# A hybrid diffusion layer on one core: the first stage in another order, with four tiles unnormalized and part of the first loads split

## The chip, the cores and the metric

The kernel runs on one core of a Trainium2 chip. The core has five engines with queues of their own: TensorE (PE in the profile, with its weight loads as PEld), VectorE (DVE), ScalarE (ACT), GpSimd (POOL) and SyncE (SP), which issues nearly all the loads. Sixteen DMA engines move the data. The metric is the device time of one execution, in microseconds. The kernel before takes 1244.59 us, the median of 3 runs (1243.99 to 1247.25).

## What is computed

One layer of a diffusion backbone over 512 latent tokens (`x`, 512 × 1024) and 256 context tokens, in float32. Its first part, which is all that the change touches, is the modulated RMS norm and the product of its result with columns of one wide matrix `w_in`:

```
def rmsnorm(x, g):
    y = x32 * lax.rsqrt(jnp.mean(x32 * x32, axis=-1, keepdims=True) + EPS)
    return y * g

def modulate(x, g, shift, scale):
    return rmsnorm(x, g) * (1 + scale) + shift

mod = jax.nn.silu(c) @ w_mod[l] + b_mod[l]            # 6 x 1024 numbers: shift, scale, gate, twice
sh1, sc1, gt1, sh2, sc2, gt2 = jnp.split(mod[:, None, :], N_MOD, axis=-1)
h_lat = modulate(x, norm1_g[l], sh1, sc1)
p_lat = h_lat @ w_in                                  # and the same for the context, with c_ctx
```

The rest (a bidirectional Mamba-2 scan, windowed attention, two branch gates, an output projection, a convolutional feed-forward network, a last RMS norm) comes after and is the same in both kernels.

## The kernel before

**Layout.** The stream is kept transposed, with channels on the 128 partitions: `x` is eight tiles of 128 channels × 512 tokens (`xs_[:, j, :]`, j from 0 to 7), the context eight tiles of 128 × 256 (`xc_`). A float32 product is made of three matmuls on rounded parts: with w = hi + lo and x = hi + lo it adds hi·hi, hi·lo and lo·hi. `split` (lines 148 to 150) makes the parts of a weight tile: a cast on ACT and a subtraction on DVE.

**The first stage** (lines 297 to 523) does three things at once. It makes shift and scale from `c` and the 8 MB of `w_mod`; it normalizes `x` and the context; and meanwhile it already multiplies `x` with the first 640 columns of the gates (`w0`, eight tiles of 128 × 640), which accumulate in five banks of PSUM, `pg[0]` to `pg[4]`.

**Unnormalized tiles.** The norm's factor r of a token is known only when the squares of all eight tiles are summed. A token's factor can be put after the product, however: with a = g·(1 + scale), h = x·a·r + s. For the first `NU` = 3 tiles, `scaled` (line 396) makes only x·a (`ah` on ACT, `al` on DVE), and the products go into the banks without r. When r is there, `scale_banks` (line 444) multiplies the five banks by it in place, on DVE, and the other tiles are added normalized (`norm`, line 388: `xsb` on DVE, `hlh` on ACT, `hll` on DVE). The shift's part of the unnormalized tiles, s·w0, is added up apart by `shifts` (line 412) in `pbias` and goes into the bias of the gates (`bias_rows`, `bias_cols`). Later products need all eight tiles normalized, so the first three are normalized too, at the end of the stage (`N0` to `N2`).

**The factor.** `squares` (line 381) squares tiles on ACT and adds them up on DVE in `ssq`, one after another. Each square is pinned (`keep_in_program_order`) behind the instruction that ACT was given just before it in the text. `sums` adds over the partitions by eight one-column matmuls on PE (line 237), adds eps on DVE, and takes the power −0.5 on POOL (line 248); `spread` spreads r over the partitions by transposes on PE (line 254), and ACT copies it into SBUF (line 273).

**The order.** PE's order is written out by hand, in the string `order`. Its words, for a tile j: `Aj` (`mod_rows`, line 352) are 16 narrow matmuls with two tiles of `w_mod`, a copy `tm` on ACT, and the split of the w0 tile j; `Bj` (`mod_cols`) are four small matmuls, after which ACT makes `a` and `s`; `Hj` (`prep`) is `scaled` or `norm`; `Pj:xy` are the products of tile j into the banks x to y−1, three matmuls each; `Zj` is `shifts`; `sq_*` are squares; `hold` and `keep` are matmuls whose result nobody reads. The other engines' queues, SP's among them, are ordered by a scheduler from the text's order and a model of the times; nothing but the pins is written by hand there.

**Loads.** SP issues the loads in the text's order. w_mod comes in 16 tiles of 512 KB in six buffers, w0 in eight tiles of 320 KB in four buffers, x in four loads of two tiles (512 KB), `vec` (all vectors by channel: 360 columns, 180 KB) in one load. Columns 0 to 55 of `vec` hold the bias of the modulation and the first norm's weights, which `a` and `s` need; columns 88 and up are read by `half` (line 445), which halves them for later stages.

After the stage, `k_step`, `q_step` and `v_step` multiply the normalized tiles (lines 193 to 196), and PE goes on without a break.

Of the kernel before, what the change touches and what calls it, by code (L numbers as in the profile page):

```python
# [20 lines left out]
L = 512  # L21
# [8 lines left out]
V_N2 = 56  # L30
V_FG = 64
V_SG = 72
V_CW = 88
# [3 lines left out]
NV = 360  # L37


def raw(ap):  # L40
    return ap.bitcast(F32)
# [3 lines left out]
def tile_hybrid_layer(  # L45
# [32 lines left out]
    nc = tc.nc  # L78
    V, S, G, T = nc.vector, nc.scalar, nc.gpsimd, nc.tensor
# [36 lines left out]
    def tmp(tag):  # L116
        return tpool.tile([P, 512], F32, tag=tag, name=tag, bufs=TMP[tag])
# [84 lines left out]
    vec = cpool.tile([P, NV], F32, name="vec")  # L202
# [9 lines left out]
    half = cpool.tile([P, NV - V_CW], F32, name="half")  # L212
# [72 lines left out]
    ssq = hpool.tile([P, L], F32, name="ssq")  # L285
# [8 lines left out]

    NU, NG = 3, 5
    first = {}
    gates = []
    with tc.tile_pool(name="spool", bufs=1) as sp:  # L300
        xs_ = sp.tile([P, KT, L], F32, name="xsb")
# [9 lines left out]
        def load_mod(i):  # L311
            t = sp.tile([P, 4, 256], F32, tag="wm", name="wm", bufs=6)
            nc.sync.dma_start(t, wm1[i].rearrange("p (k c) -> p k c", k=4))
            return t

        def load_w0(j):
            r = sp.tile([P, 640], F32, tag="w0", name="w0", bufs=4)
            nc.sync.dma_start(r, w0[j])
            return r

        def load_x(k):
            nc.sync.dma_start(xs_[:, 2 * k : 2 * k + 2, :], xT[k].rearrange("p (k t) -> p k t", k=2))

        nc.sync.dma_start(ccs, cc)
        mod_raw = {i: load_mod(i) for i in range(2)}
        nc.sync.dma_start(ident, ident_d)
        nc.sync.dma_start(vec, vecs)
        w0_raw = {0: load_w0(0)}
        load_x(0)
        for j in (1, 2):  # L330
            mod_raw.update({i: load_mod(i) for i in (2 * j, 2 * j + 1)})
            w0_raw[j] = load_w0(j)
            load_x(j)
        load_x(3)
        G.memset(raw(still), 1.0)
        G.memset(csil32, 0.0)
        G.memset(s32, 0.0)
# [43 lines left out]
        def squares(x_, q, n, ks):  # L381
            for k in ks:
                sq = tmp(("ta", "tb")[k % 2])[:, :n] if k else q
                tc.keep_in_program_order(S.activation(sq, x_[:, k, :], AF.Square))
                if k:
                    V.tensor_tensor(q, q, sq, ALU.add)
# [50 lines left out]
        def spread(x, n):  # L437
            r[x] = in_sbuf(rms_spread(r[x], n, new=accb), n, "r_" + x)

        def hold(n):  # L440
            for _ in range(n):
                T.matmul(unread[:, :256], still[:, :P], still, start=True, stop=True)

        def scale_banks():
            V.tensor_scalar_mul(half, vec[:, V_CW:NV], 0.5)
            for i in range(NG):
                V.tensor_tensor(pg[i], pg[i], r["l"], ALU.mult)

        def bias_rows():
# [15 lines left out]
        def load_next():  # L465
# [9 lines left out]
        rows = {}  # L475
# [5 lines left out]
            "N": lambda j: norm(j, 0, xs_, r["l"], hlh, hll),  # L481
        }
        calls = {
            "sq_0": lambda: squares(xs_, ssq, L, range(2)),
            "sq_1": lambda: squares(xs_, ssq, L, range(2, 4)),
            "sq_2": lambda: squares(xs_, ssq, L, range(4, 5)),
            "sq_3": lambda: squares(xs_, ssq, L, range(5, 8)),
            "hold": lambda: hold(18),
            "keep": lambda: hold(6),
            "sq_c": lambda: squares(xc_, cq, LC, range(4)),  # L490
# [2 lines left out]
            "sum_c": lambda: sums("c", cq, 2),  # L493
            "put_l": lambda: spread("l", 4),
            "put_c": lambda: spread("c", 2),
            "scale": scale_banks,
            "rows": bias_rows,
            "cols": bias_cols,
            "ctx": load_ctx,
# [2 lines left out]


        order = """
            hold A0 keep B0 H0 sq_0 keep Z0 P0:02 A1 P0:24 B1 H1 sq_1 P0:45 P1:01 A2 sq_2 P1:13 B2 H2 sq_3 P1:35 Z1 P2:01 sum_l A3
            P2:13 B3 put_l H3 P2:35 Z2 scale A4 rows ctx P3:02 B4 H4 cols P3:24 A5 sq_c P3:45 B5 H5 P4:03 A6 P4:35 B6 H6 sq_d
            P5:03 A7 N0 P5:35 B7 H7 P6:02 sum_c N1 P6:25 put_c N2 P7:05 next
        """
        with tc.manual_schedule(engines={mybir.EngineType.PE}):
            for what in order.split():  # L510
                if what in calls:
                    calls[what]()
                elif what[0] == "P":
                    j = int(what[1])
# [1628 lines left out]
```

## Time and profile before

| what | us |
|---|---|
| median of the runs | 1244.59 |
| the profiled execution | 1244.94 |
| its span, first to last instruction | 1243.1 |
| mean granted clock of TensorE | 0.996 of full |
| first product of the first stage (PE, line 409) | 10.37 |
| `sum_l` (PE, line 237) | 26.00 |
| `r_l` copied (ACT, line 273) | 32.07 |
| last products into the banks (PE, line 409), from | 59.76 |

The span is one execution, taken by the hardware profiler; the execution's own time has 1.8 us more around it. A row of the timeline gives the start, the duration, the engine, the line, the operation with the names of the output and inputs, the shapes, how many were merged (x4), and in brackets the idle time before it and who ended it. Matmuls are pipelined, so their durations overlap: the distance from one start to the next tells what one costs. The granted clock is the share of full speed at which TensorE was allowed to run in a window.

### The profile page before, as it was taken

Reading aid. Unit: us, or ns where it says so; the run is one execution under the profiler, and the core shown is the slowest. Engines: PE = TensorE matmul, PEld = TensorE weight load, DVE = VectorE, ACT = ScalarE, POOL = GpSimd, SP = SyncE. Lnnn points to the kernel's source line nnn. Section 1 sums busy time; section 2 is a strip of 40 time slices with the busy share of each in tenths; the row PEclk is TensorE's granted clock in tenths of the full one; section 3 lists DMA queues with packets and bytes.
Section 4 is the critical chain, followed back from the end, with each engine's and each line's share of the span. In section 5 each row is a group of like instructions: output and inputs, shape, how many; then the busy total and the mean of one; then the engine's idle time right before and its main releaser. Section 6 shows DMA issues by size and latency. Waiting matters only on the chain.

```text
span 1243.1 us, 17448 instructions
## 1 busy us (share of the span) xinstructions
PE 1219.0 (98%) x6322; PEld 997.8 (80%) x6322; DVE 922.0 (74%) x1482; ACT 685.5 (55%) x1302; POOL 168.9 (14%) x174
## 2 busy tenths in 40 slices
PE   8999999999999999998999999999999999999997
PEld 5798888888878877777777678888988888888885
DVE  3846887888565698697886986567688787886556
ACT  4657887888546457467375563223545444445543
POOL 0000111111100033242351630000200000000000
PEclk9999999999999999999999999999999999999998
DMA  9653568867848334446346457667154444456785
GB/s 372 224 154 87 186 197 197 229 179 208 226 153 242 114 96 125 128 133 175 125 136 220 127 185 245 197 207 240 50 170 155 145 144 153 152 171 242 246 309 184
DMA packets 108342, 224.65 MB, mean 181 GB/s; under 512 B 9440, under 2 KB 48672, under 8 KB 108256
## 3 DMA queue, kind: packets, MB, share of 16 engines
q1 hardware_dynamic: 100768, 197.32, 48.9%
q0 software_dynamic: 6912, 25.17, 8.6%
q8 instruction: 50, 0.82, 0.3%
q10 hardware_dynamic: 576, 1.05, 0.2%
q14 instruction: 36, 0.29, 0.1%
HBM read 193.29 MB, written 49.87 MB: 196 GB/s over the span
## 4 chain that ended last, share of the span: by engine, by line
PE 73%; DVE 13%; DMA 5%; ACT 5%; issue 2%; POOL 0%; SPq 0%; POOLq 0%; ACTq 0%; DVEq 0%
PE acc L193 17%; PE acc L196 17%; PE acc L194 17%; PE po L843 3%; PE score L794 3%; PE pt L830 2%; DMA wraw<-wt_d 2%; DMA wraw<-wdn 2%; PE mis L409 2%; DVE wlo L150 2%; DVE E L1450 1%; PE acc L913 1%; PE acc L915 1%; PE acc L914 1%; PE mis L1385 1%
## 5 line engine op out<-in xcount | busy, mean ns | idle before, releaser
L193 PE MATMUL acc<-hlh,whi 128*128 128x512 f32 x488 | 199.3, 408 | 0.7 <-ACT te L684 0.7
L149 ACT CAST whi<-wraw 128x1024 fp32r<-128x1024 f32 (+2 forms) x119 | 122.8, 1033 | 132.4 <-PE acc L194 94.9
L150 DVE TENSOR_TENSOR wlo<-wraw,whi 128x1024 fp32r<-128x1024 f32 (+2 forms) x119 | 143.4, 1205 | 69.4 <-ACT whi L149 64.5
L196 PE MATMUL acc<-hlh,wlo 128*128 128x512 f32 x488 | 191.4, 392 | 0.0
L194 PE MATMUL acc<-hll,whi 128*128 128x512 f32 x488 | 190.7, 391 | 0.0
L193 PE MATMUL acc<-mh,whi 128*128 128x512 f32 x360 | 141.0, 392 | 0.0
L196 PE MATMUL acc<-mh,wlo 128*128 128x512 f32 x360 | 140.1, 389 | 0.0
L194 PE MATMUL acc<-ml,whi 128*128 128x512 f32 x360 | 140.1, 389 | 0.0
L196 PEld LDWEIGHTS acc<-hlh,wlo 128*128 128x128 f32 x488 | 91.6, 188 | 20.2
L193 PEld LDWEIGHTS acc<-hlh,whi 128*128 128x128 f32 x488 | 91.9, 188 | 18.4 <-issue 2.2
L194 PEld LDWEIGHTS acc<-hll,whi 128*128 128x128 f32 x488 | 92.0, 188 | 17.5 <-issue 1.7
L194 PEld LDWEIGHTS acc<-ml,whi 128*128 128x128 f32 x360 | 67.6, 188 | 14.5 <-issue 0.5
L193 PEld LDWEIGHTS acc<-mh,whi 128*128 128x128 f32 x360 | 67.6, 188 | 14.4 <-issue 0.5
L196 PEld LDWEIGHTS acc<-mh,wlo 128*128 128x128 f32 x360 | 67.6, 188 | 14.0
L803 DVE CUSTOM_DVE_ANT_0 p<-score,winm,nsink 128x512 f32<-128x512 f32 (+1 forms) x64 | 51.8, 810 | 16.2 <-PE score L794 14.7
L1251 DVE SCALAR_TENSOR_TENSOR ta<-acc,half,ta 128x511 f32<-128x511 f32 (+1 forms) x66 | 43.8, 663 | 23.7 <-ACT ta L1250 23.7
L810 ACT ACTIVATE p<-p,mneg 128x512 f32<-128x512 f32 (+1 forms) x64 | 49.7, 777 | 15.4 <-DVE mneg L803 14.8
L1370 POOL TENSOR_TENSOR st<-st,eT 128x512 f32<-128x512 f32 x24 | 33.5, 1397 | 172.9 <-DMA wraw<-wm 106.2
L1250 ACT ACTIVATE ta<-acc,half 128x512 f32<-128x512 f32 (+1 forms) x66 | 46.6, 705 | 16.4 <-PE acc L196 15.1
L193 PE MATMUL acc<-hch,whi 128*128 128x256 f32 x176 | 54.4, 309 | 0.0
L838 DVE TENSOR_TENSOR ptl<-pt,pth 128x512 fp32r<-128x512 f32 x72 | 47.5, 685 | 8.6 <-ACT pth L834 7.8
L566 DVE SCALAR_TENSOR_TENSOR tm<-wraw,csil,tm 128x512 f32<-128x512 f32 x56 | 45.1, 805 | 10.7 <-DMA wraw<-wm 9.9
(501 smaller groups left out, 2950.4 us busy)
## 6 DMA issues: line engine op xcount, KB each, us to landing
wraw<-wup SPq DMA_DIRECT2D x44, 512.0 KB, 3.6
wt_d<-wdn POOLq DMA_DIRECT2D x36, 512.0 KB, 7.6
fb<-cs_d SPq DMA_DIRECT2D x32, 512.0 KB, 5.5
wraw<-wm SPq DMA_DIRECT2D x32, 512.0 KB, 3.6
wraw<-wx SPq DMA_DIRECT2D x24, 512.0 KB, 4.2
wraw<-wt_d SPq DMA_DIRECT2D x20, 512.0 KB, 4.2
sp_d<-te SPq DMA_DIRECT2D x33, 256.0 KB, 2.1
wm<-wm SPq DMA_DIRECT2D x16, 512.0 KB, 8.3
```

What stands on the lines that cost most here:

```text
L149: S.copy(hi[:, :n], r[:, :n])
L150: V.tensor_tensor(lo[:, :n], r[:, :n], raw(hi[:, :n]), ALU.subtract)
L193: T.matmul(ps, wh, xh[:, k0 + k, :], start=a, stop=False)
L194: T.matmul(ps, wh, xl[:, k0 + k, :], start=False, stop=False)
L196: T.matmul(ps, wl, xh[:, k0 + k, :], start=False, stop=b)
L566: V.scalar_tensor_tensor(acc, r[:, u * 512 : u * 512 + 512], sc, acc, ALU.mult, ALU.add)
L794: T.matmul(ps[:, o : o + len(z) * P], Q[h][:, b * P : (b + 1) * P], k[:, j, z[0] * P : (z[-1] + 1) * P], start=v == 0 and o % 512 in (0, P ...
L803: V.tensor_tensor_reduce(p[:, :w], d["ps"][i][:, o0 : o0 + w], m, op0=ALU.add, op1=ALU.min, scale=1.0, scalar=nsink[:, h : h + 1], accum_o ...
L810: S.activation(p, p, AF.Exp, bias=d["mneg"][:, i : i + 1], scale=-1.0, accum_out=d["den"][:, i : i + 1])
L838: V.tensor_tensor(d["ptl"][x], d["pt"][x], raw(d["pth"][x]), ALU.subtract)
L1250: S.activation(o[:, :n], ps[:, :n], AF.Identity, scale=hcol(base_w, stride + i), bias=hcol(base_b, i))
L1251: V.scalar_tensor_tensor(o[:, 1:n], ps[:, 0 : n - 1], hcol(base_w, i), o[:, 1:n], ALU.mult, ALU.add)
```

## The change

`NU` goes from 3 to 4: tile 3 is unnormalized too, has its shifts (`Z3`), and is normalized at the end (`N3`). The first two x tiles are loaded singly, the others in pairs as before; of `vec`, the first 56 columns are loaded where all were, and the rest behind the last x tile. The squares are cut otherwise (1, 1, 2 and 4 tiles instead of 2, 2, 1 and 3), and the last four, `sq_3`, stand behind `H3`. The sum `sum_l` stands behind `P3:02`, which is behind `A3`; before it stood ahead of `A3`. The scaling of the banks is in two parts, `half` is a step of its own, and the context's load (`ctx`) moves from behind `A4` to behind `A6`.

```diff
-    NU, NG = 3, 5
+    NU, NG = 4, 5
...
+        def load_tile(k):
+            nc.sync.dma_start(xs_[:, k, :], xT[k // 2, :, k % 2 * L : k % 2 * L + L])
+
         nc.sync.dma_start(ccs, cc)
         mod_raw = {i: load_mod(i) for i in range(2)}
         nc.sync.dma_start(ident, ident_d)
-        nc.sync.dma_start(vec, vecs)
+        nc.sync.dma_start(vec[:, :V_N2], vecs[:, :V_N2])
         w0_raw = {0: load_w0(0)}
-        load_x(0)
-        for j in (1, 2):
-            mod_raw.update({i: load_mod(i) for i in (2 * j, 2 * j + 1)})
-            w0_raw[j] = load_w0(j)
-            load_x(j)
+        load_tile(0)
+        mod_raw.update({i: load_mod(i) for i in (2, 3)})
+        w0_raw[1] = load_w0(1)
+        load_tile(1)
+        mod_raw.update({i: load_mod(i) for i in (4, 5)})
+        w0_raw[2] = load_w0(2)
+        load_x(1)
+        load_x(2)
         load_x(3)
+        nc.sync.dma_start(vec[:, V_N2:], vecs[:, V_N2:])
...
-        def scale_banks():
-            V.tensor_scalar_mul(half, vec[:, V_CW:NV], 0.5)
-            for i in range(NG):
+        def scale_banks(banks):
+            for i in banks:
                 V.tensor_tensor(pg[i], pg[i], r["l"], ALU.mult)
...
-            "sq_0": lambda: squares(xs_, ssq, L, range(2)),
-            "sq_1": lambda: squares(xs_, ssq, L, range(2, 4)),
-            "sq_2": lambda: squares(xs_, ssq, L, range(4, 5)),
-            "sq_3": lambda: squares(xs_, ssq, L, range(5, 8)),
+            "sq_0": lambda: squares(xs_, ssq, L, range(1)),
+            "sq_1": lambda: squares(xs_, ssq, L, range(1, 2)),
+            "sq_2": lambda: squares(xs_, ssq, L, range(2, 4)),
+            "sq_3": lambda: squares(xs_, ssq, L, range(4, 8)),
...
-            "scale": scale_banks,
+            "half": lambda: V.tensor_scalar_mul(half, vec[:, V_CW:NV], 0.5),
+            "scale_a": lambda: scale_banks(range(2)),
+            "scale_b": lambda: scale_banks(range(2, NG)),
...
         order = """
-            hold A0 keep B0 H0 sq_0 keep Z0 P0:02 A1 P0:24 B1 H1 sq_1 P0:45 P1:01 A2 sq_2 P1:13 B2 H2 sq_3 P1:35 Z1 P2:01 sum_l A3
-            P2:13 B3 put_l H3 P2:35 Z2 scale A4 rows ctx P3:02 B4 H4 cols P3:24 A5 sq_c P3:45 B5 H5 P4:03 A6 P4:35 B6 H6 sq_d
-            P5:03 A7 N0 P5:35 B7 H7 P6:02 sum_c N1 P6:25 put_c N2 P7:05 next
+            hold A0 keep B0 H0 sq_0 keep Z0 P0:02 A1 P0:23 B1 H1 sq_1 P0:35 A2 P1:02 B2 H2 sq_2 P1:25 Z1 P2:02 A3 P2:23 B3 H3 sq_3
+            P2:35 Z2 P3:02 sum_l P3:23 A4 put_l P3:34 B4 H4 P3:45 scale_a Z3 scale_b rows A5 half P4:02 cols P4:23 B5 H5 P4:35 A6 ctx sq_c P5:02 B6 H6
+            P5:24 A7 sq_d N0 P5:45 B7 H7 P6:02 sum_c N1 P6:25 put_c N2 P7:03 N3 P7:35 next
         """
```

## The prediction, on record before the changed kernel was run

> **What bounds the kernel now.** I start at the page: the span and the share of each engine.
>
> ```profile
> span 1243.1 us, 17448 instructions
> ...
> PE 1219.0 (98%) x6322; PEld 997.8 (80%) x6322; DVE 922.0 (74%) x1482; ACT 685.5 (55%) x1302; POOL 168.9 (14%) x174
> ```
>
> TensorE (PE) is busy 1219.0 of 1243.1 us, so removing every wait would save 24 us at most, and a gain made early is kept only if nothing else becomes late behind it. Next I read who waited for whom, for PE alone (total us, times, longest).
>
> ```profile
> PE mis L1278 <- DVE tc L1259: 6.0, 3, 2.4
> PE acc L237 <- DVE ssq L386: 2.1, 1, 2.1
> ```
>
> The first row is a later stage, which the change leaves alone. The second is the one large wait of the first stage: `sum_l` (line 237) waits for the last addition to the sum of squares. Then the timeline of PE there (start, duration, idle before).
>
> ```profile
> 22.36 0.63 PE L418 MATMUL acc<-w,s 128*32 128x256 f32 x6
> 22.91 0.50 PE L409 MATMUL mis<-ah,w0h 128*128 128x512 f32 x1
> 23.25 0.39 PE L409 MATMUL mis<-al,w0h 128*128 128x512 f32 x1
> 23.48 0.40 PE L409 MATMUL mis<-ah,w0l 128*128 128x512 f32 x1
> 26.00 1.02 PE L237 MATMUL acc<-rmsc,ssq 128*128 128x1 f32 x8 [2.12 <-DVE ssq L386]
> 26.95 1.07 PE L361 MATMUL acc<-wm,csil 128*32 128x256 f32 x16
> 27.95 0.82 PE L409 MATMUL mis<-ah,w0h 128*128 128x512 f32 x2
> ```
>
> The last product of `P2:01` starts at 23.48, the next product at 27.95. Between them lie the wait, one-column sums and the narrow matmuls of A3. The windows show what follows (busy us of PE, PEld, DVE, ACT, POOL, then granted clock, DMA share, GB/s):
>
> ```profile
> 20.00:30.00 10.00, 7.88 (x52) 5.38 (x51) 5.15 (x8) 4.24 (x10) 1.02 (x1) 0.92 1.03 418
> 28.00:32.00 4.00, 4.00 (x19) 3.50 (x16) 0.00 (x0) 0.88 (x3) 0.39 (x1) 0.57 1.02 417
> 32.70:56.30 23.60, 23.44 (x161) 16.21 (x160) 22.06 (x37) 15.95 (x38) 1.62 (x1) 1.00 0.63 226
> 56.30:64.40 8.10, 8.10 (x38) 6.61 (x37) 6.62 (x16) 5.64 (x13) 0.00 (x0) 1.00 0.37 127
> ```
>
> From 28 to 32 the granted clock was 0.57: 4 × 0.43 = 1.7 us of PE's work was lost. From 32.7 on it is full and PE hardly idles, but VectorE (DVE) is nearly full too, 22.06 of 23.60 us. So before 32.7 PE waits and is slowed, and after it two engines are full.
>
> **The first tile.** Its chain on ScalarE (ACT), before:
>
> ```profile
> 8.31 0.35 ACT L372 ACTIVATE a<-acc,bp,vec 128x2 f32<-128x2 f32 x1 [0.85 <-PE acc L371]
> 8.56 0.25 ACT L373 ACTIVATE s<-acc,vec 128x2 f32<-128x2 f32 x1
> 8.71 0.72 ACT L149 CAST w0h<-w 128x640 fp32r<-128x640 f32 x1
> 9.59 0.72 ACT L400 ACTIVATE ah<-xsb,a 128x512 fp32r<-128x512 f32 x1 [0.16 <-DMA xsb<-xT]
> ```
>
> The change takes 152 KB of vectors and 256 KB of x out of the queue ahead of the first x tile, 1.0 us at 417 GB/s. But `ah` idled only 0.16 us for x: it stands behind `a`, `s` and `w0h`, and `a` waited for PE. So the first product, which follows the end of `ah` at 10.31, starts 0.16 us earlier, near 10.2 (1.0 at the most, if `w0h` went first).
>
> **The load that comes next.** A3 needs w_mod tiles 6 and 7. Tile 7, before (its issue, then its time to landing):
>
> ```profile
> L313 SPq DMA_DIRECT2D wm<-wm x1: 327/327/327, 14.1 to 14.1; - x1
> ...
> DMA to landing us min/median/max: 10.5/10.5/10.5
> ```
>
> It landed at 14.1 + 10.5 = 24.6, with the DMA engines full (share 1.03 above). The new order puts the same bytes ahead of it: every x tile and both parts of `vec` are still issued first. SP issues two DMAs more, and the first vectors come in rows of 224 bytes; both cost nothing as long as PE is at A3 before the load. What PE needs until then I price by the chain that ended last:
>
> ```profile
> 46.30 0.34 PE acc L371 x4
> 46.64 2.21 PE mis L409 x9
> 48.85 1.00 PE acc L361 x16
> ```
>
> A product costs 0.245, an A 1.0, a B 0.35, and six shift matmuls 0.55 (22.36 to 22.91 above). Ahead of A3 now stand P0, P1 and `P2:02`, 36 products, 8.8; A1 and A2 2.0; B1 and B2 0.7; Z1 0.55; and 0.4 in the first tile, whose low half comes late: 12.45. PE is ready at 10.2 + 12.45 = 22.7 and waits until **24.6**. The earlier first tile, be it 0.16 or 1.0 us, is swallowed there. A3 moves from 26.95 to 24.6: **−2.35**. Behind A3 now stands `sum_l` (1.0), and 3 products (0.74) have gone ahead of it: **+0.3**. Z3 is new: **+0.55**.
>
> **The sum of squares.** Each square is pinned behind the instruction that ACT was given before it, so the first of `sq_3` stands behind `ah` of H3. In the kernel before, four additions stood behind `ah` of H2 in the same way:
>
> ```profile
> 20.42 0.50 PE L371 MATMUL acc<-sel,tm 128*128 128x2 f32 x4
> ...
> 21.35 0.72 ACT L400 ACTIVATE ah<-xsb,a 128x512 fp32r<-128x512 f32 x1
> ...
> 25.16 0.69 DVE L386 TENSOR_TENSOR ssq<-ssq,tb 128x512 f32<-128x512 f32 x1
> ```
>
> From B2 (20.42) over `ah` and the last addition to `sum_l` (26.00) it took 5.58 us, however busy PE was. After, B3 comes at 24.6 + 1.0 + 0.74 = 26.35, so `sum_l` can start at 31.9. PE has B3 0.35, `P2:35` 1.47, Z2 0.55 and `P3:02` 1.47 to do and is there at 30.2. So **a wait returns, 1.7 us**, where 2.3 went. Its length is set by the way B3, H3, squares, additions, not by the load. Ends: 0 if the squares came before `ah`, 2.3 as before.
>
> **The clock.** The stretch without a wide product was 23.7 to 27.95, 4.2 us. There are now two, 22.7 to 25.6 (2.9) and 30.2 to 32.9 (2.7). I take it that neither halves the clock: **−1.7** (ends 0 and −1.7). An A behind products, 1.0 us without a wide one (48.85 above), leaves the clock full (1.00 from 32.7 on), so the point lies between 1.0 and 4.2; 2.9 is inside, and this is rival 1. [...]
>
> **Where the factor is used.** Rows of the timeline, then of the view of the x tiles (ns min/median/max):
>
> ```profile
> 32.07 0.59 ACT L273 COPY r_l<-acc 128x512 f32<-128x512 f32 x1 [0.41 <-PE acc L254]
> ...
> 33.36 1.29 DVE L447 TENSOR_TENSOR mis<-mis,r_l 128x512 f32<-128x512 f32 x2
> ```
>
> ```profile
> L391 DVE SCALAR_TENSOR_TENSOR xsb<-xsb,a,r_l x8: 744/745/751, 32.7 to 53.4; 128x512 f32<-128x512 f32 x8
> L392 ACT ACTIVATE hlh<-xsb,s x8: 707/724/726, 33.6 to 54.3; 128x512 fp32r<-128x512 f32 x8
> L393 DVE SCALAR_TENSOR_TENSOR hll<-xsb,s,hlh x8: 743/744/752, 34.6 to 55.3; 128x512 fp32r<-128x512 f32 x8
> ```
>
> `sum_l` 31.9 to 32.9, three products, A4 to 34.65, `put_l` some 0.4, and the copy of 0.59 half a microsecond later: `r_l` is there at 36.15, against 32.66. B4 starts at 35.05 + 0.74 = 35.8 and a4, 0.9 later (B2 at 20.42 to `ah` at 21.35), is ready at 36.7. PE comes to `P4:02` after `P3:45` 0.74, Z3 0.55, A5 1.0: 38.45. One bank is scaled first (0.645), then `xsb` 0.745 to 37.55, `hlh` to 38.3, in time; `hll` stands behind another bank and ends at 39.1 to 39.75, where the second two products want it at 38.95: 0.2 to 0.8, I take **+0.5**. `half` (0.3 us) and the two parts of the scaling otherwise lie beside products.
>
> **The end of the stage.** What DVE does behind `r_l` stays the same (22.06 us of the window), less one split of 0.82, which now goes ahead, plus `half` 0.3: 21.5. It begins 3.5 us later, so it cannot end before 36.15 + 21.5 = 57.7, where it ended at 56.3; with the 1.5 us of idle as before, 59.2. The context tiles need 8.1 us more (third row to fourth), less the 0.6 they waited there: 66.7. The products of the context began at
>
> ```profile
> 65.24 0.28 PE L193 MATMUL acc<-hch,whi 128*128 128x256 f32 x1
> 65.36 0.28 PE L194 MATMUL acc<-hcl,whi 128*128 128x256 f32 x1
> ```
>
> and start 0.12 us apart, three for a tile, so the eighth tile was wanted at 65.24 + 7 × 0.36 = 67.8, and 1.0 us earlier by the sum so far: 66.8. The cover that was 3.4 us wide (64.4 to 67.8) is gone to nothing. Cost 0 to 1.5 us, I take **+0.3**, as the sums meet almost exactly. N3 is no new work: the same three instructions were H3's; only `ah` and `al` of the fourth tile are new, before `r_l`, where DVE has room (5.15 of 10 us in the first window). On SP the context's load now stands behind that of w0 tile 7, whose buffer Z3 frees only at 37.4, and ahead of w_mod tiles 14 and 15: 2368 KB at 417 GB/s are 5.8 us, 43.2, while A7 comes near 47.7 (from 38.45 on: 27 products, cols, A6, B5, B6 and the 0.5), so 4.5 us of cover are left for its landing. Behind the stage the same products follow, so I carry the shift to the end.
>
> **Sum.** −2.35 + 0.3 + 0.55 + 1.7 − 1.7 + 0.5 + 0.3 = −0.7 us. The profiled execution took 1244.94 us around its span of 1243.1; the median of the runs shown is 1244.59. I set −0.7 against the median: **1243.9 us**. About 0.3%, 3.7 us, is what a measurement of this kernel can tell from no change.
>
> **Rivals.**
> 1. *The clock is halved again.* For it: two stretches of nearly 3 us, close to each other. Against: both are shorter than the 4.2 us that did it. It decides if 2.7 to 2.9 us without wide products are enough. Price 1.7 us for one stretch, 1245.6, or 3.4 for both, 1247.3: slower than before.
> 2. *The load is no bound.* If w_mod tile 7 landed by 22.7, A3 would not wait, 1.9 less: 1242.0. Against: the same bytes ahead of it at a full share. For: the landing is that of the last of 16 engines, which need not lag as far again.
> 3. *The second wait does not come.* If ACT takes the squares before `ah` of H3 (the x tiles are long there), 1.7 less: 1242.2. Against: the pin. Under 2 or 3 the factor comes earlier, and the +0.5 and +0.3 may go too; both together give 1239.5.
> 4. *`half` blocks DVE*, which runs its queue in order. Before, it ran 26 us ahead of its place in the text (beside the scaling at 33.36):
>
> ```profile
> 7.44 0.30 DVE L445 TENSOR_SCALAR half<-vec 128x272 f32<-128x272 f32 x1
> ```
>
> The rest of `vec` now lands two w_mod tiles and one w0 tile ahead of 24.6; 1344 KB at 418 GB/s are 3.3 us, so 21.3. If `half` stands ahead of `al` of tile 1 on DVE, that `al` ends at 21.3 + 0.3 + 0.75 = 22.35 instead of near 17, PE's second products of P1 come 5.2 us late, of which the 1.9 us of slack at A3 take a part: 3.3, and 1.7 for the clock after such a gap: 1248.9, slower. Against: the square of x tile 4 stands before H2 in the text and went behind it, so the order did not count on that tile landing early.
>
> That the first rows come earlier and bring nothing is not a rival but part of the forecast.
>
> **Chances.** The forecast 0.45 (1242.5 to 1245.2, from the ends of the +0.5, the +0.3 and the 5.58 us); rival 1 0.23; rival 2 0.13; rival 3 0.12; rival 4 0.07. Faster by over 0.3%, below 1240.9, are the halves of rivals 2 and 3 in which the other terms go too: 0.14. Slower, above 1248.3, are rival 4 (0.06) and the part of rival 1 in which more than two windows are slow (0.04): 0.10. Within: 0.76. The range takes in both prices of rival 1 and leaves out rival 4 and the lower part of 2 and 3: 1240.5 to 1247.3.
>
> **What would show it.** In the profile after: A3's first matmul near 24.6 with a wait for `wm` (wrong if it starts by 23.2); a wait of `sum_l` for `ssq` near 30 to 32 of 1.7 us; a granted clock of 1.00 from 22 to 36 (rival 1: a stretch of 0.5); `r_l` near 36 and `xsb` of tile 4 at 36.8; DVE full from 36 to 59; the first context product near 64. The first product near 10.2. `half` on DVE behind `al` of tile 2. I would be wrong altogether if products behind the stage, not the stage, moved by more than a microsecond.

## The result and the profile after

| what | before, us | after, us |
|---|---|---|
| median of 6 runs each | 1245.08 | 1256.88 |
| lowest and highest | 1243.99, 1247.25 | 1251.23, 1257.38 |
| the profiled execution, its span, its mean granted clock | 1244.94, 1243.1, 0.996 | 1251.23, 1249.0, 0.995 |
| first product of the first stage | 10.37 | 10.41 |
| `sum_l` | 26.00 | 31.84 |
| `r_l` copied, from | 32.07 | 35.28 |
| `sum_c` | 53.13 | 57.05 |
| first context product (line 193) | 65.24 | 71.04 |

The changed kernel is slower: the ratio of the times, taken over all runs, is 1.0082, with an interval from 1.0063 to 1.0102 (the quotient of the two medians alone is 1.0095; the ratios below are taken over all runs too). The forecast was 1243.9 with a range up to 1247.3, so the time lies 9.6 us above that range.

Two facts say where to look. In the profiled executions the first context product moved by 71.04 − 65.24 = 5.80 us and the span by 1249.0 − 1243.1 = 5.9: what stands behind the stage took 1177.9 us before and 1178.0 after, so in these two executions the loss is in the first stage. And the profiled execution of the changed kernel is the shortest of its six. The others have spans of 1251.7 to 1255.2 at a mean clock of 0.990 to 0.992; span times clock is 1242 to 1244 in all six. So most of what the median lost beyond this profile is lost clock, not longer waits.

The page after:

```profile
span 1249.0 us, 17457 instructions
...
PE 1221.5 (98%) x6328; PEld 997.9 (80%) x6328; DVE 921.9 (74%) x1483; ACT 686.7 (55%) x1303; POOL 168.7 (14%) x174
```

PE is busy 2.5 us more (1219.0 before), for a span 5.9 us longer. Line numbers of the stage are 7 higher than before in what follows (416 was 409, 393 was 386); the helper's line 237 is the same, and later stages are 8 higher (1286 was 1278). The waits of PE after (total us, times, longest):

```profile
PE mis L1286 <- DVE tc L1267: 6.5, 3, 2.4
PE acc L237 <- DVE te L393: 4.3, 1, 4.3
PE acc L237 <- DVE ssq L393: 2.0, 1, 2.0
```

The third row is the wait at `sum_l` that the forecast said would return. The second is new: `sum_c`, the sum over the context's squares, waits 4.3 us for its last addition. Before, `sum_c` did not wait. PE's timeline at both places:

```profile
23.41 0.64 PE L368 MATMUL acc<-wm,csil 128*32 128x256 f32 x8
24.35 0.64 PE L368 MATMUL acc<-wm,csil 128*32 128x256 f32 x8 [0.30 <-DMA wm<-wm]
24.92 0.50 PE L416 MATMUL mis<-ah,w0h 128*128 128x512 f32 x1
...
31.84 1.02 PE L237 MATMUL acc<-rmsc,ssq 128*128 128x1 f32 x8 [1.98 <-DVE ssq L393]
...
52.08 0.63 PE L416 MATMUL mis<-hlh,w0l 128*128 128x512 f32 x2
57.05 0.98 PE L237 MATMUL acc<-rmsc,te 128*128 128x1 f32 x4 [4.33 <-DVE te L393]
57.89 1.63 PE L416 MATMUL mis<-hlh,w0h 128*128 128x512 f32 x3
...
71.04 0.28 PE L193 MATMUL acc<-hch,whi 128*128 128x256 f32 x1
```

and the same word before:

```profile
53.13 0.50 PE L237 MATMUL acc<-rmsc,te 128*128 128x1 f32 x4
```

PE was ready for `sum_c` at 57.05 − 4.33 = 52.72, against 53.13 before: up to here the change had gained 0.4 us. Then it waited 4.33. Why the addition was late is read from ACT and DVE. ACT after:

```profile
50.04 0.38 ACT L370 COPY tm<-acc 128x256 f32<-128x256 f32 x1 [0.36 <-PE acc L368]
50.31 1.05 ACT L149 CAST whi<-wraw 128x1024 fp32r<-128x1024 f32 x1
51.26 0.73 ACT L149 CAST w0h<-w 128x640 fp32r<-128x640 f32 x1
51.88 0.42 ACT L391 ACTIVATE ta<-xcb 128x256 f32<-128x256 f32 x1
...
52.82 0.40 ACT L391 ACTIVATE tb<-xcb 128x256 f32<-128x256 f32 x1
```

ACT before:

```profile
48.84 0.40 ACT L384 ACTIVATE ta<-xcb 128x256 f32<-128x256 f32 x1
...
49.76 0.40 ACT L384 ACTIVATE tb<-xcb 128x256 f32<-128x256 f32 x1
```

These are the first and the last of the four squares of `sq_d`. The new order has it behind `A7`, where it was ahead of `P5:03 A7`, and each square is pinned behind the instruction that stands before it in ACT's text. So the first is now pinned behind the cast `w0h` of A7, which itself comes behind the copy `tm` that waits for A7's matmuls (50.04), and it starts 51.88 − 48.84 = 3.04 us later. DVE after:

```profile
51.44 1.22 DVE L150 TENSOR_TENSOR wlo<-wraw,whi 128x1024 fp32r<-128x1024 f32 x1
52.57 0.82 DVE L150 TENSOR_TENSOR w0l<-w,w0h 128x640 fp32r<-128x640 f32 x1
53.31 0.42 DVE L393 TENSOR_TENSOR te<-te,ta 128x256 f32<-128x256 f32 x1
53.64 0.74 DVE L398 SCALAR_TENSOR_TENSOR xsb<-xsb,a,r_l 128x512 f32<-128x512 f32 x1
54.30 0.42 DVE L393 TENSOR_TENSOR te<-te,tb 128x256 f32<-128x256 f32 x1
54.64 0.74 DVE L400 SCALAR_TENSOR_TENSOR hll<-xsb,s,hlh 128x512 fp32r<-128x512 f32 x1
55.30 0.42 DVE L393 TENSOR_TENSOR te<-te,ta 128x256 f32<-128x256 f32 x1
55.81 0.75 DVE L400 SCALAR_TENSOR_TENSOR hll<-xsb,s,hlh 128x512 fp32r<-128x512 f32 x1
56.48 0.42 DVE L393 TENSOR_TENSOR te<-te,tb 128x256 f32<-128x256 f32 x1
```

DVE before, its last of the four:

```profile
51.22 0.43 DVE L386 TENSOR_TENSOR te<-te,tb 128x256 f32<-128x256 f32 x1
```

DVE is full here: two splits (1.22 and 0.82) stand ahead of the first addition, where before `wlo` stood behind the last, and the four additions of 0.42 stand among norm steps of 0.74. The last one ends at 56.90 against 51.65 before, 5.25 later: 3.04 from ACT's queue and 2.2 from DVE's. Before, 1.48 us of cover lay between that end and `sum_c` (51.65 to 53.13). PE now comes 0.41 earlier, and 0.15 pass from the last addition to `sum_c` (56.90 to 57.05): 5.25 − 1.48 + 0.41 + 0.15 = 4.33, the wait. What then happens to the clock (busy us of PE, PEld, DVE, ACT, POOL, then granted clock, DMA share, GB/s):

```profile
52.00:54.00 2.00, 0.71 (x4) 0.23 (x2) 2.00 (x4) 2.00 (x7) 0.00 (x0) 1.00 0.23 35
54.00:56.00 2.00, 0.00 (x0) 0.00 (x0) 1.91 (x5) 1.78 (x3) 0.00 (x0) 0.75 0.59 211
56.00:58.00 2.00, 0.95 (x5) 0.98 (x5) 2.00 (x3) 0.00 (x0) 0.00 (x0) 0.50 0.00 0
58.00:60.00 2.00, 2.00 (x6) 1.61 (x6) 0.41 (x4) 0.00 (x0) 0.71 (x1) 0.50 0.41 72
60.00:62.00 2.00, 2.00 (x8) 1.43 (x7) 0.00 (x0) 0.00 (x0) 0.00 (x0) 0.55 0.46 182
62.00:64.00 2.00, 2.00 (x12) 1.64 (x10) 1.32 (x4) 1.17 (x3) 0.00 (x0) 1.00 0.00 0
```

The clock falls while PE idles and stays at half until about 61.8, of which 57.05 to 61.8 is work: some 2.4 us lost. So the profile's account of the stage is −0.4 (to `sum_c`) + 4.33 (wait) + 1.9 (what remains by the first context product, clock less small changes) = 5.8. The clock behind `sum_l`, which the forecast counted as kept, was full in this execution:

```profile
28.00:32.00 4.00, 2.02 (x13) 1.24 (x8) 3.48 (x6) 2.07 (x4) 0.00 (x0) 1.00 0.93 327
32.00:36.00 4.00, 4.00 (x37) 2.88 (x37) 0.27 (x2) 0.96 (x2) 1.02 (x1) 1.00 0.94 336
```

### The profile page after: what moved, and what is told of

Its sections match the earlier page's. It is cut to its first block, busy times and chain, and to the rows that moved or that the text cites. A ratio compares the mean times of both kernels' runs of the same rounds, so it can differ in the third digit from the quotient of the medians.

```text
span 1249.0 us, 17457 instructions
## 1 busy us (share of the span) xinstructions
PE 1221.5 (98%) x6328; PEld 997.9 (80%) x6328; DVE 921.9 (74%) x1483; ACT 686.7 (55%) x1303; POOL 168.7 (14%) x174
## 3 DMA queue, kind: packets, MB, share of 16 engines
q10 hardware_dynamic: 576, 1.05, 0.2%
## 4 chain that ended last, share of the span: by engine, by line
PE 74%; DVE 10%; DMA 8%; ACT 4%; issue 2%; SPq 0%; POOL 0%; POOLq 0%; ACTq 0%; DVEq 0%
PE acc L193 17%; PE acc L196 17%; PE acc L194 17%; DMA wraw<-wt_d 3%; PE po L851 3%; PE score L802 3%; PE pt L838 2%; DMA wm<-wm 2%; DMA wraw<-wdn 1%; PE mis L1376 1%; DVE E L1458 1%; PE acc L921 1%; DVE wlo L150 1%; PE acc L923 1%; PE acc L922 1%
```

## The experiments

The theory: the loss is `sq_d`'s place in ACT's queue, and the clock that falls in the wait it makes. The rivals: DVE is full and 3.5 us later behind the new `r_l`, so `sum_c` would wait wherever the squares stand; the split loads; the late context load; the clock behind `sum_l`. The context load is settled by the trace of the changed kernel: it was issued at 31.5 and 32.0 and landed by 38.6, and the first square of the context started at 44.1 without a wait for it. All runs, each compared with the kernel before on the same chip in the same job:

| run | change | median, us | before, us | ratio | interval |
|---|---|---|---|---|---|
| `e1_sqd_early` | after, `sq_d` ahead of P5 | 1247.97 | 1244.49 | 1.0026 | 1.0013 to 1.0038 |
| `e4_before_sqd_late` | before, `sq_d` behind A7 | 1250.33 | 1244.49 | 1.0039 | 1.0025 to 1.0053 |
| `e2_fill` | after, unread matmuls in `sum_c`'s wait | 1252.90 | 1244.49 | 1.0070 | 1.0044 to 1.0095 |
| `e3_again` | after, one execution | 1253.86 | 1244.49 | | |
| `e8_fill_l` | e1, unread matmuls in `sum_l`'s wait | 1245.33 | 1245.08 | 1.0003 | 0.9989 to 1.0017 |
| `e11_fill_both` | after, unread matmuls in both waits | 1248.99 | 1243.71 | 1.0037 | 1.0021 to 1.0053 |
| `e12_before_fill` | before, unread matmuls in its wait | 1243.12 | 1243.71 | 0.9990 | 0.9976 to 1.0003 |
| `e5_before_loads` | before, the split loads alone | 1242.98 | 1245.08 | 0.9997 | 0.9983 to 1.0011 |
| `e6_sq3_early` | e1, `sq_3` ahead of A3 | 1242.30 | 1245.08 | 0.9983 | 0.9968 to 0.9998 |
| `e7_sum_early` | e6, `sum_l` ahead of Z2 | 1242.48 | 1245.08 | 0.9982 | 0.9965 to 1.0000 |
| `e10_old_loads` | e6 with the loads of before | 1243.37 | 1244.22 | 0.9990 | 0.9977 to 1.0004 |
| `e9_x_late` | e6, x tiles 4 to 7 behind w_mod tile 7 | 1246.87 | 1244.22 | 1.0019 | 1.0005 to 1.0033 |

### The place of `sq_d`

It is undone in the changed kernel,

```diff
-            P5:24 A7 sq_d N0 P5:45 B7 H7 P6:02 sum_c N1 P6:25 put_c N2 P7:03 N3 P7:35 next
+            sq_d P5:24 A7 N0 P5:45 B7 H7 P6:02 sum_c N1 P6:25 put_c N2 P7:03 N3 P7:35 next
```

> The changed kernel with sq_d ahead of P5:24, as it stood in the kernel before (ahead of A7). Theory A (late squares): the last four context squares are pinned behind A7's split, their additions end 4.3 us after PE is at sum_c, and the clock halves after the gap. Then sum_c's wait goes below 0.5 us, the clock stays at 1.00 from 50 to 66, the profiled span falls from 1249.0 by 4.3 + 2.3 to 1242 to 1243, and the runs stop scattering (1251 to 1257 before). Theory B (full VectorE): the factor comes 3.2 us later than before, VectorE is full whatever the place, and the additions are late anyway: sum_c still waits 2 us or more and the span stays above 1245.

and done alone in the kernel before:

```diff
-            ... P4:35 B6 H6 sq_d
-            P5:03 A7 N0 P5:35 B7 H7 P6:02 sum_c N1 P6:25 put_c N2 P7:05 next
+            ... P4:35 B6 H6
+            P5:03 A7 sq_d N0 P5:35 B7 H7 P6:02 sum_c N1 P6:25 put_c N2 P7:05 next
```

> The kernel before, with sq_d alone moved from behind H6 to behind A7. Theory A: sum_c waits some 3 us and the clock halves behind it: 1248 to 1251. Theory B: VectorE has room in the kernel before, so the wait is below 1 us and the time stays within 1 us of 1244.6.

Waits of PE, of the first and of the second:

```profile
PE acc L237 <- DVE te L393: 1.1, 1, 1.1
```

```profile
PE acc L237 <- DVE te L386: 3.4, 1, 3.4
```

Undone, the wait falls from 4.3 to 1.1, the first context product goes from 71.04 to 66.61, and the median from 1256.88 to 1247.97. Done alone, it makes a wait of 3.4 in a kernel with the old loads, the old three tiles and the old `sum_l`, and costs 0.4% (0.25 to 0.53), inside what was expected. Both agree on the cause. In e1 neither theory's numbers came: a wait of 1.1 lies between the 0.5 of the one and the 2 of the other, the profiled span was 1244.5, and the runs still scatter by 4.3 us (6.2 in the changed kernel). The 1.1 us that stays goes with the rival, the full DVE: in e1 `r_l` is copied at 35.66, 3.6 us later than before, and in e6 and e7 below, where it is copied at 33.06 and 31.86, the wait is 0.75 and nothing. That is three points of kernels that differ in more than this, so it is argued, not shown. And e1 at +0.26% is still not the forecast −0.7 us; the clock behind `sum_l`, next, is a part of that.

### The clock in the two waits

`e2_fill` puts 34 matmuls whose result nobody reads ahead of `sum_c`, so that PE is busy in the wait; `e3_again` is the changed kernel itself beside it.

```diff
+        def fill(n):
+            for _ in range(n):
+                T.matmul(pmod[:, :256], still[:, :P], still, start=True, stop=True)
...
-            P5:24 A7 sq_d N0 P5:45 B7 H7 P6:02 sum_c N1
+            P5:24 A7 sq_d N0 P5:45 B7 H7 P6:02 fill sum_c N1
```

> The changed kernel with 34 matmuls that nobody reads (about 4.2 us) ahead of sum_c, so that PE is busy through the wait; nothing else moves. Theory A1 (a wait and then the clock, and the scatter of the runs is the clock): the wait's 4.3 us stay, the half clock behind it goes: span 1249.0 - 2.3 = 1246.7, runs 1248 to 1250 without the 1257 ones. Theory A2 (the clock is no part of it, or the slow runs come from elsewhere): the span stays at 1249 and the runs still reach 1257.

> The changed kernel as it is, for a second profile: the runs lie at 1251, 1254 and 1257, the first profile at 1251. Theory A1: a longer execution has the same waits and more time at half clock behind sum_l or sum_c, 1.7 us of work lost for each 3.4 us. Theory A2: it has another wait or a later landing.

The fill kept the clock at 1.00 from 50 to 66 us, but it ended too late: it writes to the tile that A7 and B7 use, and waited 0.95 us for ACT to read `s` from it, and `sum_c` came at 59.92, 0.9 us after its last addition. Neither theory held as a whole: the profiled span was 1250.8, not 1246.7 or 1249, and one run of five still took 1257.8. The median of 1252.9 is 4 us under that of the changed kernel, but the two intervals overlap, so e2 by itself shows the clock in the trace and no sure gain in time. Its profile also lost 1.7 us of clock behind `sum_l` (33.6 to 37.0), as did the next one. `e3_again` met the first of its two theories: it has the same waits, and it showed what the profile of the changed kernel above had not. Its windows behind `sum_l`:

```profile
32.00:36.00 4.00, 4.00 (x32) 2.49 (x31) 0.16 (x1) 0.37 (x1) 1.02 (x1) 0.74 1.01 387
36.00:40.00 4.00, 4.00 (x34) 2.69 (x32) 2.39 (x4) 2.51 (x6) 0.00 (x0) 0.83 1.02 359
```

The program is the same and so are its waits (1.97 at `sum_l`, 4.33 at `sum_c`), yet here the clock was halved behind `sum_l` too, at a price of 4 × 0.26 + 4 × 0.17 = 1.7 us. Its first context product came at 73.22, 2.2 later than in the other profile of this kernel. A further 1.7 us of clock went at a later place, behind a wait for `tc` at 508 us, where the other profile shows 1.00; the span is 2.7 us longer.

`e8_fill_l` fills `sum_l`'s wait in e1 (16 matmuls, 2.1 us), `e11_fill_both` fills both in the changed kernel (16 and 24):

```diff
+            "fill": lambda: hold(16),
...
-            P2:35 Z2 P3:02 sum_l P3:23
+            P2:35 Z2 P3:02 fill sum_l P3:23
...
-            ... P6:02 sum_c N1
+            ... P6:02 fill_c sum_c N1
```

The last two lines are e11's alone; `fill_c` is the `fill` of e2 with 24.

> e1 (sq_d early) with 16 matmuls that nobody reads, about 2 us, ahead of sum_l, in its wait of 2.0 us. Theory A1 (e1's runs scatter from 1246 to 1250 because the clock sometimes halves behind the 2.9 us without wide products at sum_l): the runs gather near the fastest of e1, 1246 to 1247, and no profile shows half clock from 32 to 40. Theory A2 (the scatter comes from elsewhere): median and scatter stay, 1248 and 1246 to 1250.

> The changed kernel with matmuls whose result nobody reads ahead of both sums: 16 (2.1 us) ahead of sum_l, 24 (3.0 us, of the 0.126 us each that 34 took before) ahead of sum_c. The waits stay as long as they are, only PE is busy in them. Theory A (the loss is the time of the two waits and the clock that falls behind them, nothing else): the granted clock is 1.00 from 20 to 70 us, the first context product stands near 68.2 (66.6 with sq_d early, plus 4.3 - 1.1 of wait, less what the sum_l clock took in no profile there, and 1.5 us less if DVE's delay is partly covered, so 68 to 70), and the median is 1245.3 (sq_d early with the sum_l wait filled) + 3.3 = 1248.6, 1247.5 to 1250. Theory B (the wait also makes later work late, on DVE and ACT, or the clock falls for another reason): above 1251, with waits or a lowered clock behind 62 us.

`e11_fill_both`, windows around `sum_c`:

```profile
50.00:54.00 4.00, 3.37 (x25) 2.19 (x17) 4.00 (x7) 3.65 (x9) 0.00 (x0) 1.00 0.02 4
54.00:58.00 4.00, 3.43 (x27) 3.26 (x27) 3.90 (x9) 2.44 (x5) 0.00 (x0) 1.00 0.41 123
58.00:62.00 4.00, 4.00 (x21) 3.26 (x21) 1.82 (x7) 0.69 (x2) 0.70 (x1) 1.00 0.40 123
```

In e11 the last addition ends at 57.56, 0.7 later than in the changed kernel, and `sum_c` comes at 57.71, but the clock is 1.00 from 20 us to 70. It is slower than before by 5.3 us where the changed kernel is slower by 11.8: so by the medians some 6.5 of the 11.8 are clock (by the ratios, 0.82% and 0.37%, it is 5.6), and the rest is mostly the time of the waits. The expectation of 1248.6 was met (1248.99), and so was that of the first context product (69.53). e8 against e1, 1245.33 to 1247.97, puts the share of the clock behind `sum_l` at 2.6 us of the median; the two stem from different jobs and the intervals of their ratios overlap, so this size is supported, not settled. What e8 did not do is gather the runs, as its first theory said: they scatter by 4.8 us, from 1243.3 to 1248.1, no less than in e1 (4.3). So the scatter comes from other places too.

`e12_before_fill` does the same in the kernel before, ahead of its `sum_l`:

```diff
-            ... B2 H2 sq_3 P1:35 Z1 P2:01 sum_l A3
+            ... B2 H2 sq_3 P1:35 Z1 P2:01 fill sum_l A3
```

> The kernel before with 16 unread matmuls (2.1 us) ahead of sum_l, in its wait of 2.1 us; sums and narrow matmuls behind them are as before. If the stretch without wide products set the clock of 0.57 at 28 to 32 us, the clock stays at 1.00 there and the kernel gains up to 1.7 us: 1242.8 against a median before near 1244.5 (ratio 0.9986), unless the fill itself delays sum_l by more than 0.3 us. If narrow matmuls behind the wait halve it by themselves, or DVE then is the bound behind 32.7 and takes the gain back, no change.

```profile
28.00:32.00 4.00, 4.00 (x28) 3.07 (x28) 0.73 (x2) 1.87 (x5) 0.57 (x1) 1.00 1.03 419
```

The clock of 0.57 in these microseconds is 1.00 now, and the first context product comes at 63.81, 1.4 earlier. In the median it is 0.6 us, inside what can be told from nothing: the profiled execution lost more than the gain again at three later places (see the last section).

The profiles taken together say more than the medians. Eight of them have an unfilled wait of 1.6 to 2.2 us at `sum_l`, and in six (before, e2, e3, e4, e5, e9) the clock was halved behind it, at a price of 1.7 to 3.4 us; three (after, e3, e4) have an unfilled wait of 3.4 to 4.3 us at `sum_c`, and in all three it was, at the same price. Of the five waits that were filled (e2, e8, e12, and both in e11), none was followed by a clock under 1.00.

### The loads, and the first sum

`e5_before_loads` is the kernel before with the split loads of x and `vec`, as they stand in the diff of the change:

```diff
-        nc.sync.dma_start(vec, vecs)
+        nc.sync.dma_start(vec[:, :V_N2], vecs[:, :V_N2])
...
-        load_x(0)
+        load_tile(0)
...
+        nc.sync.dma_start(vec[:, V_N2:], vecs[:, V_N2:])
```

`e10_old_loads` is `e6_sq3_early` with the same lines the other way round. `e6` puts the four squares `sq_3` ahead of A3, so that they no longer stand behind `ah` of H3 on ACT; `e7` also takes `sum_l` and `put_l` ahead:

```diff
-            ... P1:25 Z1 P2:02 A3 P2:23 B3 H3 sq_3
+            ... P1:25 Z1 P2:02 sq_3 A3 P2:23 B3 H3
             P2:35 Z2 P3:02 sum_l P3:23 A4 put_l ...
-            P5:24 A7 sq_d N0 ...
+            sq_d P5:24 A7 N0 ...
```

```diff
-            P2:35 Z2 P3:02 sum_l P3:23 A4 put_l P3:34
+            P2:35 sum_l Z2 P3:02 P3:23 put_l A4 P3:34
```

> The kernel before with the changed loads alone: the first two x tiles singly, the first 56 columns of the vectors first and the rest behind the last x tile. Theory A (as forecast: the first rows bring nothing): the first product starts within 0.3 us of 10.37, sum_l stays at 26.0 within 0.7 us because the chain B2, H2, squares, additions sets it, and the median stays within 0.1% of the kernel before. Rival: tile 0 a microsecond earlier carries through to sum_l, 1 us faster.

> The changed kernel with sq_d ahead of P5:24 (as in e1) and sq_3 ahead of A3 instead of behind H3, so that the last four squares of x are pinned behind sq_2 and not behind ah of tile 3. Theory A (the 2.0 us at sum_l come from the pin behind H3): the wait is below 0.3 us, the factor comes 2 us earlier, sum_c's wait of 1.07 us goes with it, and the runs no longer fall to half clock behind sum_l: median 1248.0 - 2 - 1 to 2 for the clock, 1243.5 to 1245. Theory B (the load is late: x tiles 6 and 7 land too late, or VectorE is the limit): the wait stays above 1 us and the median above 1246.

> e6 with sum_l moved from behind P3:02 to behind P2:35 and put_l from behind A4 to ahead of it: the factor comes some 3 us earlier than in e6, work on PE the same. Theory A (in e6 VectorE is still full behind the factor and holds up tiles 4 to 7 and the context): the waits of P4:02, P5:02 and sum_c go, 1 to 2 us faster than e6, 1242 to 1243.5. Theory B (with the squares early VectorE has room again): the same as e6 within 0.5 us.

> e6 (sq_d ahead of P5:24, sq_3 ahead of A3) with the loads of the kernel before: x in four pairs, the vectors in one load. Theory A (the earlier first rows are swallowed by the wait for w_mod tile 7, which the same bytes stand ahead of): A3's second half starts at 24.3 to 24.7 in both, the first context product within 0.4 us of e6's 63.7, the median within 0.1% of e6's 1242.3. Rival (the split loads are what makes e6 faster): 1 us or more slower than e6.

`e6`, timeline of PE:

```profile
24.32 0.64 PE L368 MATMUL acc<-wm,csil 128*32 128x256 f32 x8 [0.58 <-DMA wm<-wm]
...
29.68 0.95 PE L237 MATMUL acc<-rmsc,ssq 128*128 128x1 f32 x8
...
51.94 0.58 PE L237 MATMUL acc<-rmsc,te 128*128 128x1 f32 x4 [0.75 <-DVE te L393]
...
63.73 0.28 PE L193 MATMUL acc<-hch,whi 128*128 128x256 f32 x1
```

With the squares ahead of `ah`, `sum_l` waits for nothing, as the first theory said, the clock is full from 24 to 66, and the first context product comes 1.5 us earlier than in the kernel before. The wait at `sum_c` did not go, as that theory also said: 0.75 is left. At 0.9983 (0.9968 to 0.9998) this version is clearly faster than the changed kernel and at best a little faster than the one before: the interval ends close to 1, and e10, the same order with the old loads, reaches 1.0004. e7, whose stage ends another 0.7 earlier (63.04), has the same median, as its second theory had it. The split loads bring nothing that these runs can tell: e5 is at 0.9997, with `sum_l` at 25.52 and its first product at 10.02, just outside the 0.3 us that were expected, and e10 against e6 has the first context product at 63.51 against 63.73.

`e9_x_late` takes the x tiles 4 to 7 and the rest of `vec` out of the queue ahead of w_mod tile 7:

```diff
-        load_x(2)
-        load_x(3)
-        nc.sync.dma_start(vec[:, V_N2:], vecs[:, V_N2:])
...
-            ... P2:02 sq_3 A3 P2:23
+            ... P2:02 A3 late sq_3 P2:23
```

> e6 with the last two pairs of x and the rest of the vectors loaded behind w_mod tiles 6 and 7, 1.2 MB less ahead of A3, and sq_3 behind A3. Theory A (w_mod tile 7's landing holds A3): A3 runs without a wait from about 22.7, 1.5 us earlier than in e6; but the squares then go behind ah of tile 3 in ACT's order, so a wait at sum_l comes back, 1.5 to 2 us, and the first context product is within 1 us of e6's 63.7. Rival (A3's wait is not the bytes ahead of it): A3 still ends near 24.9.

A3 then started at 22.82 without a wait, so the load of tile 7 was what A3 waited for. But the squares came behind `ah` of tile 3, as expected, and `sum_l` waited 2.19 at 30.95. Behind that wait the clock stood at 0.50 from 31.5 to 38.3, 3.4 us lost, `r_l` was copied at 36.72 where e6 has 33.06, and the first context product came at 68.94, 5 us behind e6. The expected 63.7, within 1 us, was wrong: it had the wait, and left out the clock behind it.

## Why the prediction failed

**Right, with sizes.** The earlier first rows are swallowed (first product 10.41, forecast 10.2; over the ten profiles with the split loads it lies at 9.8 to 10.5, over the four without at 10.4 to 10.5; e5 and e10 show no gain). A3 does wait for `wm`, but only 0.30 us: PE was there at 23.41, not 22.7, and its first eight matmuls use tile 6, which is there earlier, a split that the sum had not made. So A3 ended at 24.92 where 25.6 was forecast. The wait at `sum_l` returned, 1.98 at 31.84 (forecast 1.7 at 31.9), through the pin behind `ah`, as e6 shows by taking it away. That the time fits to 0.1 us is luck: B3 came at 25.72, 0.6 earlier than forecast, and the way from it to `sum_l` took 6.12, 0.5 longer than the 5.58 taken over from before, because a split `w0l` (0.82 at 30.27) now ran on DVE ahead of the last addition. `r_l` was done at 35.87 (forecast 36.15), and `P4:02` waited 0.4 for `hll` (forecast 0.5). `half` ran at 22.44, behind `al` of tile 2, so rival 4 did not come. Rival 3 did not come either; rival 2 came in part, as the load held A3 for 0.3 us instead of 1.9. The context's load was issued from 31.5 on, not behind 37.4 as the sum had it, and cost nothing. Behind the stage nothing moved in the pair of profiles above.

**The step that failed: "The end of the stage", +0.3.** It priced the cover of the context's *normalized* tiles and the landing of the context's load. It did not price the change's own move of `sq_d` from ahead of `P5:03` to behind A7, which stands in the diff and not in the description of the change: four squares pinned behind one more cast on ACT, four additions on a DVE that the same paragraph called full, and `sum_c` on PE waiting for the last of them. Every number for it stood in the trace of before: the additions ended at 51.65 and `sum_c` came at 53.13, so 1.5 us of cover, against a `w0h` of 0.7 and a `whi` of 1.05 that now run ahead of the squares, and a queue on DVE on top. In place of +0.3 the profile shows 4.33 of wait and 1.9 of clock, together 6.2 against the 0.3 forecast; e1 takes most of it away and e4 makes it in the kernel before.

**The term that was mis-sized: the clock, −1.7.** The forecast took it that neither of two stretches of nearly 3 us halves the clock, with rival 1 for the case that they do. Both happen, with the same program: full clock in the profile above, half behind `sum_l` in `e3_again`. So that gain is there in some executions only, and rival 1 came in part; the new gap at `sum_c` brought another stretch of half clock, twice as long, that neither the forecast nor the rival had. `e3_again` halves the clock after a wait of 1.97 and 1.0 us of one-column sums, and with three wide products behind them; in the first profile of the changed kernel the same stretch without a wide product, 29.9 to 32.7, leaves it at 1.00. So its length alone does not decide; that there is a point between 1.0 and 4.2 us was an estimate.

**Do the terms add up?** To about a microsecond, and the runs tell no more. Without the +0.3 the terms come to −1.0 us; in the changed kernel PE was ready for `sum_c` at 52.72 against 53.13, which is −0.4, and 0.28 of the difference is a wait for `hlh` at 45.14 that the forecast did not have. With the wait at `sum_c` of e1 (1.07) the −1.0 becomes +0.1. e8, which has that wait and the clock kept behind `sum_l`, measured +0.25 in the median, but the interval of its ratio reaches from −1.4 to +2.1 us, and in its profile the first context product came at 66.56, 1.3 later than before. What the forecast lacked, beside these smaller errors, is the wait for `sq_d` and the clock behind both waits.

**What stays open.** None of the executions near 1257 was profiled. Their mean clock of 0.990 to 0.991 against 0.995 is worth about 0.0045 × 1250 = 5.6 us of span, and their spans are 5.6 to 6.2 longer; that these are stretches of the same kind, as in `e3_again`, is argued and not shown, and where in the program they lie is open.

## What to carry to other kernels

When a step is moved by name, follow each of its instructions to the queue that it lands in: here a move of one word put four squares behind a cast on ACT and four additions into a full DVE, and PE, nine products later, waited 4.3 us. A moved producer is priced against the cover its consumer had (here 1.5 us), not against the work it stands beside. Where the waits stayed, matmuls that nobody reads kept the clock at 1.00 here (`e11_fill_both`, 20 to 70 us), but the 34 of `e2_fill` were too many: `sum_c` came 0.9 us after its last addition. Better is to move the producer ahead of what it is pinned behind, as e6 does (1242.30 against 1245.08 before).

## What was not expected of the hardware

The half clock came in pieces of one length, 3.4 us, or of twice that length. Windows of `e1_sqd_early` and of the kernel before, around a later wait for `tc` (2.16 us in e1, 2.41 in the kernel before):

```profile
500.00:510.00 10.00, 8.37 (x47) 7.84 (x48) 6.37 (x9) 6.21 (x13) 2.54 (x2) 0.83 0.57 179
```

```profile
500.00:510.00 10.00, 9.47 (x58) 8.44 (x59) 5.61 (x9) 5.32 (x11) 1.44 (x2) 1.00 0.75 218
```

10 × 0.17 = 1.7 us are lost in the one, none in the other, at the same place of the program, and the shorter wait is the one that lost. A loss of 1.7 us at half clock is a stretch of 3.4 us. The same 1.7 stands behind `sum_l` in the kernel before (4 × 0.43), in `e3_again`, and three times in `e12_before_fill`, at 498 to 504 and in two more windows that show 1.00 in the kernel before:

```profile
560.00:570.00 10.00, 8.22 (x38) 6.02 (x33) 9.39 (x16) 9.01 (x26) 3.92 (x4) 0.83 0.59 196
670.00:680.00 10.00, 8.18 (x32) 6.63 (x33) 4.96 (x8) 4.85 (x8) 0.00 (x0) 0.83 0.87 291
```

Behind `sum_c` in the changed kernel the stretch is twice as long, 54 to 62: 2 × (0.25 + 0.50 + 0.50 + 0.45) = 3.4 lost. It is so behind `sum_l` too in `e5_before_loads` and `e9_x_late`, after waits of only 1.57 and 2.19 us. From the first product to the end of the matmuls the clock of the kernel before is at half once, from 28.45 to 31.86, which is 3.41 us; that of the changed kernel once, from 54.99 to 61.81, 6.83 us. In the twelve other profiles the windows up to 880 us show, at each place where the clock falls, a loss of 1.7 or of 3.4 us, and in e6, e7, e10 and e11 none; those that lie wholly in such a place show 0.50.

The same wait in the same program is followed by half a clock in one execution and not in another. In `e3_again` `sum_l` starts at 31.84, after 1.97 us of wait, the three wide products at 32.72 and A4 at 33.61, and the clock falls only near 33.9 (by the 4 × 0.26 lost up to 36), when PE has worked for 2.1 us again. In the first profile of the changed kernel the three start at 31.84, 32.72 and 33.59, after 1.98 us of wait, and the clock stays at 1.00. So PE need not idle up to the fall. What decides between the two is not shown, and how much work keeps the clock was not tried. If each wait of some 2 us costs 1.7 us or nothing, three such losses, as many as the profile of `e12_before_fill` shows, make 5 us, the size of the scatter among the runs of one program; that is an estimate, and which waits cost it in which run was not tried.
